# Token halves of 272 and 240 instead of 256 and 256 at the layer boundaries and around the layer norm, in a kernel of two fused transformer blocks

## The chip, the cores and the metric

The kernel runs on one core of one Trainium2 chip. The metric is the time of one execution on the device in microseconds, as the median of several runs. The engines are TensorE (PE in the profile; its weight loads are PEld), VectorE (DVE), ScalarE (ACT), GpSimd (POOL) and SyncE (SP, whose queue carries most of the DMA).

## What is computed

512 tokens of width 1024 pass through two blocks of layers. The first block has two layers, each of them a mixer and a squared-ReLU MLP with an RMS norm before and after ("sandwich"); the mixer of layer 0 is a gated short convolution beside a multi-head attention, that of layer 1 a convolution module with a layer norm inside. The second block is one layer with another attention, pooling and a gated MLP.

```python
for i in range(DEPTH):
    g = sandwich_gains[i]
    h = rms_norm(x, g[0])
    m = parallel_conv_mla(h, ...) if i % 2 == 0 else conformer_conv(h, ...)
    x = x + rms_norm(m, g[1])
    h = rms_norm(x, g[2])
    x = x + rms_norm(squared_relu_mlp(h, mlp_w1[i], mlp_w2[i]), g[3])

def conformer_conv(h, w_pw1, b_pw1, w_dw, b_dw, ln_g, ln_b, w_pw2, b_pw2):
    a, g = jnp.split(h @ w_pw1 + b_pw1, 2, axis=-1)
    u = depthwise_conv(a * jax.nn.sigmoid(g), w_dw) + b_dw
    return jax.nn.silu(layer_norm(u, ln_g, ln_b)) @ w_pw2 + b_pw2
```

What matters here is the line `x = x + rms_norm(m, g)`, followed by the next norm and the next matrix product. It occurs four times, after each mixer and each MLP of the first block. Everything is in float32.

## The kernel before

Activations lie transposed: a tile has 128 channels on its partitions and the 512 tokens along its free dimension, eight tiles to a tensor. A float32 product is made of three matmuls on numbers split into a rounded high part and the rest: high weights by high and low activations, low weights by high activations (`mm3`, L357 to L359). So each activation tile is split before it is used (`split`: ScalarE writes the high part, L397 or, with a scale, L400; VectorE writes the rest, L398 or L401), and so is each block of four 128x128 weight tiles, which arrives as `raw` by DMA and is copied by ScalarE (L284) and subtracted by VectorE (L286; by GpSimd for one stretch of blocks) into a `W` buffer.

The four joints between the layers of the first block are written once, in `boundary`. There the mean of squares over the 1024 channels of `m` is needed for every token before `x` can be updated, and the updated `x` before the next layer's products can start. The tokens are therefore cut in two halves, `LA` (L58) and `LB` (L63), of 256 each:

- The last three output tiles of the old layer (`tile`) are made for LA first, 72 matmuls, then for LB. Each tile is evacuated from PSUM by the caller's `evac` (after the MLPs VectorE adds, L1058; after the mixers ScalarE copies, L923 or L1219) and squared; the squares of the first two are added to `acc` (L469 on ScalarE, L470 on VectorE), the square of the third stays by itself (L949).
- `sums` adds over the channels with three matmuls: the high part of `acc` (L962), its low part (L963), and the third tile's square (L964, a plain float32 matmul, which the profile shows as two rows). It stands for LA after five of the eight products of the first LB tile, and for LB inside the next layer's first pass, in `hook`.
- `rsqrt` makes the scale of a half (L450 on ScalarE, L420, L422 and L424 on VectorE).
- `update` multiplies m by it (L970 on VectorE) and adds it to x (L973, on GpSimd for all of LA, and for LB on VectorE for tiles 0, 1, 2 and 4); `update2` splits the new x into `h` (L400 on ScalarE, L401 on VectorE).
- The next layer's first four output tiles are made in two passes of 96 matmuls, k outermost (`kouter`): the LA pass, which after k = 2 (`HK`) runs `hook`, so that the sum over LB stands there on TensorE, and then the LB pass.

The conformer's layer norm and the products behind it use the same halves (L1175 to L1222), and so does the last output tile of the kernel (L1688).

Each engine works its own queue off in order and waits on semaphores where it needs another. The program is recorded in the order of the code, and the tile framework's scheduler, which weighs the instructions by their shapes, then sets the order of each engine's queue; so what stands next to what on VectorE and ScalarE at a boundary is not in the code.

Of the kernel before, what the change touches and what calls it, by code (L numbers as in the profile page):

```python
# [54 lines left out]
XA = ()  # L55
XB = (0, 1, 2, 4)
HK = 2
LA = slice(0, 256)  # L58
TABLES = [s.name for s in SETS]
EXP_LN, LN = "natural_log_exp_and_others", "natural_log"  # L60
RSQRT, TRIG = "abs_reciprocal_sqrt_and_small", "trig_and_small"
SIGMOID, SILU = "sigmoid_and_others", "silu_and_others"
LB = slice(256, 512)  # L63

# [173 lines left out]

class Weights:
# [58 lines left out]
class Program:  # L304
# [624 lines left out]
    def boundary(self, x, m, acc, last, gi, nxt, first, extra=None):  # L929
# [5 lines left out]
        V, A, G, mm = nc.vector, nc.scalar, nc.gpsimd, nc.tensor.matmul  # L935
        self.norm_set = RSQRT
        self.tables(RSQRT)
        r, acc2 = self.S()[:, :T], self.S()[:, :T]
        h = []
        sq = {}  # L940

        def evac(i, ps, cols):
            o, _, f = last[i]
            f(ps[:, cols], o, cols)
            if i < 2:
                self.square_into(acc[:, cols], m[o][:, cols], False)
            else:
                sq[0] = self.S()[:, :256]
                A.activation(out=sq[0], in_=m[o][:, cols], func=AF.Square)  # L949

        def tile(i, cols, part=slice(0, None), ps=None):
            ps = ps or self.PS()
            for f in last[i][1][part]:
                f(ps[:, cols], cols)
            return ps

        def parts(cols):
            return self.split(self.P(), acc[:, cols], cols=256), sq[0]

        def sums(p, s):  # L960
            ps = self.PS()[:, :256]
            mm(ps, self.ones, p[:, 0, :256], start=True, stop=False)  # L962
            mm(ps, self.ones, p[:, 1, :256], start=False, stop=False)  # L963
            mm(ps, self.onesf, s, start=False, stop=True)  # L964
            return ps

        def update(k, cols):
            if cols is LA:
                h.append(self.P())
            V.scalar_tensor_tensor(out=m[k][:, cols], in0=m[k][:, cols], scalar=self.v("g", 8 * gi + k),  # L970
                                   in1=r[:, cols], op0=OP.mult, op1=OP.mult)
            eng = V if k in (XA if cols is LA else XB) else G
            ins = eng.tensor_add(out=x[k][:, cols], in0=x[k][:, cols], in1=m[k][:, cols]).ins  # L973
            if eng is G:
                self.last_update = ins
# [5 lines left out]
        def updates(ks, cols):  # L981
            ks = list(ks)
            update(ks[0], cols)
            for a, b in zip(ks, ks[1:] + [None]):
                if b is not None:
                    update(b, cols)
                update2(a, cols)

        for i in range(3):
            ps = tile(i, LA)  # L990
            evac(i, ps, LA)
        pb = [tile(0, LB, slice(0, 5))]
        s = sums(*parts(LA))
        tile(0, LB, slice(5, None), pb[0])
        self.rsqrt(s, D, r[:, LA])
        updates(range(4), LA)
        for i in (1, 2):
            pb.append(tile(i, LB))
        for i in range(3):
            evac(i, pb[i], LB)  # L1000
        box = {"p": parts(LB)}

        def hook():
            box["s"] = sums(*box["p"])
            updates(range(4, 8), LA)
            self.rsqrt(box["s"], D, r[:, LB])
            updates(range(8), LB)
            for k in range(8):
                self.square_into(acc2[:, LA], x[k][:, LA], k == 0, G)
            for k in range(8):  # L1010
                self.square_into(acc2[:, LB], x[k][:, LB], k == 0)

        ps = self.kouter(first, h, None, LA, {HK: hook}, extra and extra[0], range(8))
# [50 lines left out]
    def conformer(self, x, h, ps4, rs, first):  # L1064
        nc = self.nc
        V, A, G, mm, W = nc.vector, nc.scalar, nc.gpsimd, nc.tensor.matmul, self.W
# [105 lines left out]
        self.tables(RSQRT)  # L1172

        order = LN_ORDER
        mean = [self.PS()[:, :256] for _ in range(2)]  # L1175

        def means(i):
            for c in order:
# [1 line left out]

        means(0)
        h2 = [self.P() for _ in range(8)]
        sq = [self.PS()[:, :256] for _ in range(2)]
        mus = {}

        def squares(i, cs):
            cols = (LA, LB)[i]
            if i not in mus:
                mus[i] = self.S()[:, :256]
                A.activation(out=mus[i], in_=mean[i], func=AF.Copy, scale=1.0 / D)  # L1190
            for c in cs:
                V.tensor_sub(out=vv[c][:, cols], in0=vv[c][:, cols], in1=mus[i])
                t = self.S()[:, :256]
                A.activation(out=t, in_=vv[c][:, cols], func=AF.Square)
                mm(sq[i], self.onesf, t, start=c == 0, stop=c == 7)

        def normal(i):
            cols = (LA, LB)[i]
            r = self.S()[:, :256]
            self.rsqrt(sq[i], D, r)  # L1200
            self.tables(SILU)
            for c in range(8):
                y = vv[c][:, cols]
                V.tensor_mul(out=y, in0=y, in1=r)
                self.fn(SILU, out=y, in_=y, func=AF.Silu, scale=self.v("lng", c), bias=self.v("lnb", c))
                self.split(h2[c], y, cols=cols)
# [536 lines left out]
```

## Time and profile before

| | |
|---|---|
| median of 3 runs | 1763.58 us (1763.04 to 1767.39) |
| the profiled execution | 1762.84 us |
| its span, first to last instruction | 1761.1 us |
| mean granted TensorE clock | 0.991 |
| TensorE busy | 1724.0 us (98% of the span) |
| VectorE, ScalarE, GpSimd busy | 1091.2, 801.6, 274.0 us |
| share of TensorE in the chain that ended last | 81% |

The times of all rows are microseconds from the start of the span, of the one profiled execution. A row of the timeline gives the start, the duration, the engine, the line, the operation with its output and inputs, the shape, and in brackets the idle time ahead of it with the instruction that ended it. Durations of matmuls contain the way through the array, so neighbours overlap; what a matmul costs is read from the distance of the starts. The four boundaries lie at about 229 to 265, 586 to 623, 794 to 830 and 1152 to 1190 us.

### The profile page before, as it was taken

The numbers are of one execution on the slowest core, as the hardware profiler recorded it, in microseconds if no ns is written. First come the engines' busy times: TensorE is split into PE (matmuls) and PEld (weight loads), VectorE is DVE, ScalarE is ACT, GpSimd is POOL, SyncE is SP. The second block draws the span as 40 slices with busy tenths as digits, with TensorE's granted clock in tenths as the row PEclk, the third lists the DMA queues.
The fourth block names the chain that finished last, engine by engine and source line by source line (L and its number), as shares of the span: only waits on it lengthen the run. The fifth ranks groups of instructions, "written<-read, shape, count | busy, mean of one in ns | idle before, by whom it ended". The sixth has DMA issues, their size and how long they took to land.

```text
span 1761.1 us, 23142 instructions
## 1 busy us (share of the span) xinstructions
PE 1724.0 (98%) x8828; PEld 1460.4 (83%) x8828; DVE 1091.2 (62%) x1772; ACT 801.6 (46%) x1461; POOL 274.0 (16%) x339
## 2 busy tenths in 40 slices
PE   9999999999999999999999999989999999999999
PEld 7778898888888878999888888888787888888887
DVE  7988786344444789968544444488897655344452
ACT  6546655333333446676533333357665443232331
POOL 3513330000000365503000000051223200000000
PEclk9999999999999999999999999999999999999999
DMA  5231313222222133512322222222223222222221
GB/s 198 73 104 55 108 51 130 96 96 96 96 96 96 48 108 107 169 60 85 109 97 96 96 96 96 96 96 74 73 62 101 100 97 98 96 96 96 96 96 60
DMA packets 49887, 167.26 MB, mean 95 GB/s; under 512 B 6848, under 2 KB 7296, under 8 KB 49776
## 3 DMA queue, kind: packets, MB, share of 16 engines
q1 hardware_dynamic: 47776, 160.70, 27.9%
q0 software_dynamic: 1936, 5.07, 0.9%
q8 instruction: 69, 1.13, 0.3%
q14 instruction: 42, 0.34, 0.1%
q10 hardware_dynamic: 64, 0.02, 0.0%
HBM read 158.25 MB, written 4.19 MB: 92 GB/s over the span
## 4 chain that ended last, share of the span: by engine, by line
PE 81%; DVE 11%; issue 3%; ACT 2%; POOL 2%; DMA 1%; SPq 0%; POOLq 0%; ACTq 0%; DVEq 0%
PE ps L357 26%; PE ps L358 26%; PE ps L359 26%; DVE P L970 1%; PE ps L625 1%; DVE W L286 1%; POOL P L973 1%; DVE P L401 1%; DVE S L1479 1%; DVE S L424 1%; DVE P L398 1%; DVE S L422 1%; DMA raw<-in_w 1%; ACT S L450 0%; DVE S L420 0%
## 5 line engine op out<-in xcount | busy, mean ns | idle before, releaser
L357 PE MATMUL ps<-P,W 128*128 128x512 f32 (+1 forms) x2541 | 928.7, 366 | 4.9 <-DVE S L1132 2.8
L358 PE MATMUL ps<-P,W 128*128 128x512 f32 (+1 forms) x2541 | 925.7, 364 | 4.9 <-DVE P L401 4.9
L359 PE MATMUL ps<-P,W 128*128 128x512 f32 (+1 forms) x2541 | 923.9, 364 | 0.0
L284 ACT ACTIVATE W<-raw 128x512 fp32r<-128x512 f32 x578 | 356.6, 628 | 649.9 <-PE ps L359 608.5
L286 DVE TENSOR_TENSOR W<-raw,W 128x512 fp32r<-128x512 f32 x523 | 371.0, 717 | 378.7 <-ACT W L284 376.1
L357 PEld LDWEIGHTS ps<-P,W 128*128 128x128 f32 x2541 | 482.6, 190 | 82.5 <-DVE S L1132 3.2
L358 PEld LDWEIGHTS ps<-P,W 128*128 128x128 f32 x2541 | 482.7, 190 | 79.9 <-DVE P L401 5.7
L359 PEld LDWEIGHTS ps<-P,W 128*128 128x128 f32 x2541 | 482.6, 190 | 75.3 <-DVE W L286 0.2
L973 POOL TENSOR_TENSOR P<-P 128x256 f32<-128x256 f32 x48 | 46.7, 981 | 770.6 <-DVE P L970 769.5
L398 DVE TENSOR_TENSOR P<-S,P 128x512 fp32r<-128x512 f32 (+3 forms) x134 | 93.8, 706 | 50.4 <-ACT P L397 49.8
L397 ACT ACTIVATE P<-S 128x512 fp32r<-128x512 f32 (+3 forms) x134 | 81.5, 614 | 63.8 <-DVE S L1666 25.9
L286 POOL TENSOR_TENSOR W<-raw,W 128x512 fp32r<-128x512 f32 x55 | 72.9, 1348 | 38.1 <-ACT W L284 34.0
L1084 DVE SCALAR_TENSOR_TENSOR ps<-P,vec,ps 128x512 f32<-128x512 f32 x116 | 77.8, 744 | 0.0
L400 ACT ACTIVATE P<-P,vec 128x256 fp32r<-128x256 f32 (+1 forms) x80 | 43.7, 550 | 51.8 <-POOL P L973 31.4
L1031 DVE SCALAR_TENSOR_TENSOR S<-ps,S 128x512 f32<-128x512 f32 x64 | 43.6, 689 | 34.2 <-PE ps L359 34.1
L401 DVE SCALAR_TENSOR_TENSOR P<-P,vec 128x256 fp32r<-128x256 f32 (+1 forms) x80 | 54.3, 692 | 10.9 <-ACT P L400 10.7
L470 POOL TENSOR_TENSOR S<-S 128x256 f32<-128x256 f32 (+1 forms) x45 | 48.7, 1084 | 74.6 <-ACT S L469 72.2
L469 ACT ACTIVATE S<-P 128x256 f32<-128x256 f32 (+1 forms) x105 | 46.4, 472 | 17.4 <-DVE P L1058 11.4
L638 POOL TENSOR_TENSOR P<-S,P 128x512 fp32r<-128x512 f32 (+1 forms) x24 | 34.3, 1427 | 114.4 <-DVE P L637 108.5
L1051 DVE TENSOR_TENSOR P<-ps,P 128x512 f32<-128x512 f32 x42 | 29.0, 691 | 28.7 <-PE ps L359 28.7
L625 PE MATMUL ps<-P 128*128 128x512 f32 (+3 forms) x160 | 41.2, 376 | 2.2 <-DVE S L1445 0.9
L470 DVE TENSOR_TENSOR S<-S 128x256 f32<-128x256 f32 (+1 forms) x60 | 33.1, 551 | 14.4 <-ACT S L469 13.4
(264 smaller groups left out, 1299.8 us busy)
## 6 DMA issues: line engine op xcount, KB each, us to landing
raw<-in_w SPq DMA_DIRECT2D x286, 512.0 KB
P<-in_xT SPq DMA_DIRECT2D x8, 256.0 KB
P<-in_xT POOLq DMA_DIRECT2D x8, 256.0 KB, 5.3
keep<-P SPq DMA_DIRECT2D x8, 256.0 KB
P<-P SPq DMA_DIRECT2D x16, 128.0 KB
P<-keep POOLq DMA_DIRECT2D x8, 256.0 KB, 4.3
out<-P SPq DMA_DIRECT2D x7, 256.0 KB
raw<-in_w SPq DMA_DIRECT2D x2, 256.0 KB
```

The costliest lines, as they stand in the source:

```text
L284: nc.scalar.activation(out=w[:, 0, :cols], in_=r, func=AF.Copy)
L286: eng.tensor_sub(out=w[:, 1, :cols], in0=r, in1=w[:, 0, :cols].bitcast(F32))
L357: mm(ps, w[0], x[0], start=first, stop=False)
L358: mm(ps, w[0], x[1], start=False, stop=False)
L359: mm(ps, w[1], x[0], start=False, stop=last)
L397: nc.scalar.activation(out=hi, in_=src, func=AF.Copy)
L398: nc.vector.tensor_sub(out=lo, in0=src, in1=hi.bitcast(F32))
L401: nc.vector.scalar_tensor_tensor(out=lo, in0=src, scalar=scale, in1=hi.bitcast(F32), op0=OP.mult, op1=OP.subtract)
L470: (eng or nc.vector).tensor_add(out=acc, in0=acc, in1=t)
L625: mm(o[:m], k, q[:, pl, c0:], start=n == 0 and m == 128, stop=n == len(keys) - 1 and mask is None)
L973: ins = eng.tensor_add(out=x[k][:, cols], in0=x[k][:, cols], in1=m[k][:, cols]).ins
L1084: V.scalar_tensor_tensor(out=dst if dst is not None and t == taps[-1] else acc, in0=u, scalar=w, in1=acc, op0=OP.mult, op1=OP.add)
```

## The change

LA takes 272 tokens and LB 240. The widths that were written as 256 follow from the slices, by a new function `size`. It adds four lines above the code of interest, so that a line n of the profile is n + 4 in the changed kernel.

```diff
-LA = slice(0, 256)
+LA = slice(0, 272)
-LB = slice(256, 512)
+LB = slice(272, 512)
...
+def size(cols):
+    return cols.stop - cols.start
...
             else:
-                sq[0] = self.S()[:, :256]
+                sq[0] = self.S()[:, :size(cols)]
...
         def parts(cols):
-            return self.split(self.P(), acc[:, cols], cols=256), sq[0]
+            return self.split(self.P(), acc[:, cols], cols=size(cols))[:, :, :size(cols)], sq[0]
 
         def sums(p, s):
-            ps = self.PS()[:, :256]
-            mm(ps, self.ones, p[:, 0, :256], start=True, stop=False)
-            mm(ps, self.ones, p[:, 1, :256], start=False, stop=False)
+            ps = self.PS()[:, :s.shape[-1]]
+            mm(ps, self.ones, p[:, 0], start=True, stop=False)
+            mm(ps, self.ones, p[:, 1], start=False, stop=False)
             mm(ps, self.onesf, s, start=False, stop=True)
...
-        mean = [self.PS()[:, :256] for _ in range(2)]
+        mean = [self.PS()[:, :size(cols)] for cols in (LA, LB)]
...
-        sq = [self.PS()[:, :256] for _ in range(2)]
+        sq = [self.PS()[:, :size(cols)] for cols in (LA, LB)]
...
-                mus[i] = self.S()[:, :256]
+                mus[i] = self.S()[:, :size(cols)]
...
-                t = self.S()[:, :256]
+                t = self.S()[:, :size(cols)]
...
-            r = self.S()[:, :256]
+            r = self.S()[:, :size(cols)]
```

TensorE's order stays as it was at the boundaries. The queues of VectorE and ScalarE are arranged anew at all four boundaries. Three places show it.

ScalarE at the first boundary, from the last weight copy or split ahead of the second four updates to the rsqrt of LB. `ps_2273` is the third tile's second half, `S_2307` its square, `P_2309` the split of `acc` for LB; P_2356 to P_2377 are h[4] to h[7] for LA, each of which needs its GpSimd addition. Before:

```order
L284 ACTIVATE W_2245<-raw_2158 128x512
L400 ACTIVATE P_2233<-P_1946,vec_82 128x256
L923 ACTIVATE P_1944<-ps_2273 128x256
L949 ACTIVATE S_2307<-P_1944 128x256
L397 ACTIVATE P_2309<-S_1957 128x256
L400 ACTIVATE P_2356<-P_1947,vec_82 128x256
L400 ACTIVATE P_2359<-P_1947,vec_82 128x256
L400 ACTIVATE P_2367<-P_1948,vec_82 128x256
L400 ACTIVATE P_2377<-P_1948,vec_82 128x256
L450 ACTIVATE S_2063<-ps_2352,eps_84 128x256
```

After:

```order
L401 ACTIVATE P_2309<-S_1957 128x240
L288 ACTIVATE W_2238<-raw_2121 128x512
L404 ACTIVATE P_2356<-P_1947,vec_82 128x272
L404 ACTIVATE P_2359<-P_1947,vec_82 128x272
L404 ACTIVATE P_2367<-P_1948,vec_82 128x272
L404 ACTIVATE P_2377<-P_1948,vec_82 128x272
L288 ACTIVATE W_2245<-raw_2158 128x512
L927 ACTIVATE P_1944<-ps_2273 128x240
L953 ACTIVATE S_2307<-P_1944 128x240
L454 ACTIVATE S_2063<-ps_2352,eps_84 128x240
```

The third tile's evacuation and its square have moved from ahead of the four splits into h[4] to h[7] to behind them, with two weight copies now ahead of them as well.

VectorE at the first boundary, from the end of the rsqrt of LA. P_2212 to P_2233 are h[0] to h[3]; P_1652, P_1721 and P_1906 hold m. Before:

```order
L424 SCALAR_TENSOR_TENSOR S_2063<-S_2207,S_2063 128x256
L970 SCALAR_TENSOR_TENSOR P_1652<-P_1652,vec_82,S_2063 128x256 x2
L286 TENSOR_TENSOR W_2220<-raw_2084,W_2220 128x512
L401 SCALAR_TENSOR_TENSOR P_2212<-P_1945,vec_82,P_2212 128x256
L970 SCALAR_TENSOR_TENSOR P_1721<-P_1721,vec_82,S_2063 128x256
L401 SCALAR_TENSOR_TENSOR P_2215<-P_1945,vec_82,P_2215 128x256
L286 TENSOR_TENSOR W_2230<-raw_2121,W_2230 128x512
L970 SCALAR_TENSOR_TENSOR P_1721<-P_1721,vec_82,S_2063 128x256
L401 SCALAR_TENSOR_TENSOR P_2223<-P_1946,vec_82,P_2223 128x256
L286 TENSOR_TENSOR W_2238<-raw_2121,W_2238 128x512
L286 TENSOR_TENSOR W_2245<-raw_2158,W_2245 128x512
L401 SCALAR_TENSOR_TENSOR P_2233<-P_1946,vec_82,P_2233 128x256
```

After:

```order
L428 SCALAR_TENSOR_TENSOR S_2063<-S_2207,S_2063 128x272
L974 SCALAR_TENSOR_TENSOR P_1652<-P_1652,vec_82,S_2063 128x272 x2
L974 SCALAR_TENSOR_TENSOR P_1721<-P_1721,vec_82,S_2063 128x272 x2
L405 SCALAR_TENSOR_TENSOR P_2212<-P_1945,vec_82,P_2212 128x272
L405 SCALAR_TENSOR_TENSOR P_2215<-P_1945,vec_82,P_2215 128x272
L405 SCALAR_TENSOR_TENSOR P_2223<-P_1946,vec_82,P_2223 128x272
L405 SCALAR_TENSOR_TENSOR P_2233<-P_1946,vec_82,P_2233 128x272
L474 TENSOR_TENSOR S_1957<-S_1957,S_2299 128x240
L974 SCALAR_TENSOR_TENSOR P_1906<-P_1906,vec_82,S_2063 128x272
L290 TENSOR_TENSOR W_2220<-raw_2084,W_2220 128x512
```

The four multiplications and the four low parts of LA stand together, and the weight splits that stood between them come later.

VectorE at the second boundary, around the evacuation of the second and third tile for LB (`ps_4946`, `ps_4971`); P_5007 is the split of `acc` for LB, P_5054 to P_5075 are h[4] to h[7] for LA. Before:

```order
L470 TENSOR_TENSOR S_4611<-S_4611,S_4997 128x256
L1058 TENSOR_TENSOR P_2824<-ps_4946,P_2824 128x256
L1058 TENSOR_TENSOR P_2824<-ps_4971,P_2824 128x256
L970 SCALAR_TENSOR_TENSOR P_2823<-P_2823,vec_82,S_4761 128x256
L470 TENSOR_TENSOR S_4611<-S_4611,S_5001 128x256
L970 SCALAR_TENSOR_TENSOR P_2823<-P_2823,vec_82,S_4761 128x256
L970 SCALAR_TENSOR_TENSOR P_2824<-P_2824,vec_82,S_4761 128x256
L398 TENSOR_TENSOR P_5007<-S_4611,P_5007 128x256
```

After:

```order
L1062 TENSOR_TENSOR P_2824<-ps_4946,P_2824 128x240
L474 TENSOR_TENSOR S_4611<-S_4611,S_5001 128x240
L290 TENSOR_TENSOR W_4936<-raw_4819,W_4936 128x512
L402 TENSOR_TENSOR P_5007<-S_4611,P_5007 128x240
L405 SCALAR_TENSOR_TENSOR P_5054<-P_1947,vec_82,P_5054 128x272
L405 SCALAR_TENSOR_TENSOR P_5057<-P_1947,vec_82,P_5057 128x272
L405 SCALAR_TENSOR_TENSOR P_5065<-P_1948,vec_82,P_5065 128x272
L405 SCALAR_TENSOR_TENSOR P_5075<-P_1948,vec_82,P_5075 128x272
L290 TENSOR_TENSOR W_4943<-raw_4856,W_4943 128x512
L1062 TENSOR_TENSOR P_2824<-ps_4971,P_2824 128x240
```

The third tile's evacuation has moved from ahead of the split of `acc` to behind it, the four low parts and a weight split. The third boundary is arranged like the first (with L1219 for L923), the fourth like the second.

## Rows read from the trace of the kernel before

**Rows 1.** The page: span, and TensorE's busy time, share and instructions

```profile
span 1761.1 us, 23142 instructions
...
PE 1724.0 (98%) x8828; PEld 1460.4 (83%) x8828; DVE 1091.2 (62%) x1772; ACT 801.6 (46%) x1461; POOL 274.0 (16%) x339
```

**Rows 2.** Waits of TensorE: who waited for whom; us in total, times, longest

```profile
PE ps L963 <- DVE P L398: 5.2, 4, 1.3
PE ps L358 <- DVE P L401: 4.9, 4, 2.2
PE ps L962 <- ACT P L397: 3.8, 4, 1.7
```

**Rows 3.** Timeline of TensorE at the first boundary: sum over LB, and second pass

```profile
240.65 0.39 PE L962 MATMUL ps<-P,ones 128*128 128x256 f32 x1 [0.21 <-ACT P L397]
242.33 0.39 PE L963 MATMUL ps<-P,ones 128*128 128x256 f32 x1 [1.29 <-DVE P L398]
242.56 0.90 PE L964 MATMUL ps<-S,onesf 128*128 128x256 f32 x2
242.89 0.77 PE L357 MATMUL ps<-P,W 128*128 128x256 f32 x1
...
252.99 0.39 PE L358 MATMUL ps<-P,W 128*128 128x256 f32 x1 [1.02 <-DVE P L401]
```

**Rows 4.** Stages: length, busy us and count by engine, granted clock, DMA share, GB/s

```profile
242.70:246.10 3.40, 3.40 (x17) 3.23 (x16) 2.23 (x6) 1.65 (x5) 1.07 (x2) 0.50 0.00 0
252.99:264.50 11.51, 11.51 (x96) 11.51 (x97) 11.47 (x23) 7.71 (x18) 3.81 (x4) 1.00 0.21 61
990.00:1010.00 20.00, 20.00 (x90) 16.57 (x89) 10.35 (x15) 9.32 (x16) 0.00 (x0) 1.00 0.32 105
```

**Rows 5.** Timeline of TensorE at the second and fourth boundary

```profile
601.53 0.78 PE L357 MATMUL ps<-P,W 128*128 128x256 f32 x1
...
611.12 0.39 PE L358 MATMUL ps<-P,W 128*128 128x256 f32 x1 [0.59 <-DVE P L401]
...
1178.63 0.39 PE L358 MATMUL ps<-P,W 128*128 128x256 f32 x1 [2.20 <-DVE P L401]
```

**Rows 6.** Timeline of TensorE: narrow matmuls of the second block's attention

```profile
1261.05 0.27 PE L358 MATMUL ps<-P 128*128 128x160 f32 x1
...
1261.27 0.22 PE L357 MATMUL ps<-P 128*128 128x32 f32 x1
```

**Rows 7.** Timeline of ScalarE at the first boundary

```profile
234.89 0.36 ACT L923 ACTIVATE P<-ps 128x256 f32<-128x256 f32 x1
...
236.38 0.62 ACT L284 ACTIVATE W<-raw 128x512 fp32r<-128x512 f32 x1
...
238.37 0.42 ACT L949 ACTIVATE S<-P 128x256 f32<-128x256 f32 x1
...
245.38 0.46 ACT L450 ACTIVATE S<-ps,eps 128x256 f32<-128x256 f32 x1
...
256.70 0.91 ACT L400 ACTIVATE P<-P,vec 128x256 fp32r<-128x256 f32 x2 [0.79 <-POOL P L973]
```

**Rows 8.** Timeline of VectorE at the first and second boundary

```profile
232.10 1.22 DVE L286 TENSOR_TENSOR W<-raw,W 128x512 fp32r<-128x512 f32 x1
...
239.00 0.41 DVE L470 TENSOR_TENSOR S<-S 128x256 f32<-128x256 f32 x1
239.34 0.47 DVE L970 SCALAR_TENSOR_TENSOR P<-P,vec,S 128x256 f32<-128x256 f32 x1
...
587.79 0.42 DVE L1058 TENSOR_TENSOR P<-ps,P 128x256 f32<-128x256 f32 x1
...
589.11 1.75 DVE L970 SCALAR_TENSOR_TENSOR P<-P,vec,S 128x256 f32<-128x256 f32 x3
...
594.01 1.28 DVE L286 TENSOR_TENSOR W<-raw,W 128x512 fp32r<-128x512 f32 x2
```

**Rows 9.** Timeline of GpSimd at the first boundary

```profile
231.87 2.05 POOL L973 TENSOR_TENSOR P<-P 128x256 f32<-128x256 f32 x2 [25.53 <-DVE P L970]
234.67 0.91 POOL L973 TENSOR_TENSOR P<-P 128x256 f32<-128x256 f32 x1 [0.75 <-DVE P L970]
```

## The prediction

> **What bounds the kernel now.** I read the page first. TensorE is busy for 98% of the span of 1761.1 us [rows 1], so the time moves only if a matmul takes longer or shorter, if TensorE waits, or if its clock is not granted. The list of who waited for whom comes next: three of TensorE's waits are at the four boundaries and nowhere else, 5.2 us on L963, 4.9 on L358 and 3.8 on L962, four times each, 13.9 us together [rows 2]. TensorE's timeline shows them in place. At the first boundary the column sums of the second half begin at 240.65, their second matmul waits 1.29 us for VectorE's split at L398, the next layer's matmuls go on at 242.89, and at 252.99 the first matmul that needs the second half of h[0] waits 1.02 us for L401 [rows 3]. The table by stage adds a third loss: in the 3.4 us from 242.70 the granted clock is 0.50, the lower of the two levels, right after TensorE had stood still, and 17 matmuls run where 28 fit at the spacing of the second pass (96 in 11.51 us, 0.120 each); that loses some 1.3 us [rows 4]. The second and fourth boundary look the same, with 0.59 and 2.20 us at the later wait [rows 5]; the third then has about 1.1, what is left of the 4.9.
>
> So a boundary is a chain that runs over VectorE, ScalarE and GpSimd, with TensorE waiting for it twice. What the change does to that chain decides, and the order rows show that it does more than alter widths.
>
> **The change, part by part.** *Matmul widths.* In each half 263 products of three matmuls change, so 789 get 16 columns more and 789 get 16 fewer. From 512 columns (90 in 20.00 us, 0.222 each) to 256 (0.120) a column costs 0.0004 us, 16 of them 0.0064 [rows 4]. With 272 columns that makes 0.126, with 240 it makes 0.114: the pair costs as before, and the sum is 0. One end of this: narrow matmuls have a floor, since with 160 columns they still start 0.11 apart (1261.05 to 1261.27 is two steps) [rows 6]. 0.114 lies above it. Were 240 columns no faster than 256, the second half would give nothing back, 789 x 0.0064 = +5.0 us; were they at the floor of 0.11, 789 x 0.004 = -3.2 us. I take 0, since 0.114 is nearer to the floor that is measured than to 0.120. The Trainium skill (TensorE: Matmul & The Clock Gate, section "LDWEIGHTS (loading the stationary operand)") gives a weight load as its columns over 1.2 ns, 107 ns for 128 columns; by its section "Back-to-back issue gap" 256 columns need 109 ns and 240 need 102.5, so the load would hold the narrower half, and the sum would be an estimated +3.5 us instead of 0. The measured 0.11 agrees with its floor; no row here has 240 columns.
>
> *Order at the first and third boundary.* Before, ScalarE evacuated the third tile's second half (L923) and squared it (L949) as soon as the first four updates were through, at 238.4 [rows 7], some two microseconds before TensorE began that sum. Now both stand behind four more L400, each of which needs its GpSimd addition, and two weight copies. The third matmul of the second sum reads that square, so TensorE must wait for it. Worked out from 231.87, where the first addition starts (times are those of the trace before): four additions at 0.96 (1.02 in the pair, 0.91 alone [rows 9]) end at 235.75; the fourth L400 0.51 (256.70: the next starts 0.4 later), 236.25; L923 0.36 and the square 0.42, 237.0 [rows 7]; VectorE's L470 0.41 and L970 0.47, 237.9; a weight split L286, 0.64 alone and 1.22 beside GpSimd, taken as 1.0, 238.9; three L970 beside GpSimd 1.75, 240.65; a second split 1.0 and the second L470 0.41, 242.05 [rows 8]; L397 as long as a square, 242.5; a weight copy L284 0.62, 243.1; four L400 in 1.7, 244.8; L284 0.62, L923 0.36, L949 0.42, 246.2. Neighbours in a queue overlap by up to 0.07 (L470 takes 0.41, its successor starts 0.34 later [rows 8]), over some 15 steps less 0.3 where the step is not handed to another engine: 245.9. In the old run the sum's last matmul started 0.33 before the next layer went on; so TensorE goes on at 246.25 instead of 242.89 [rows 3], **+3.4 us**. The ends: with every split alone and additions at 0.91 the square ends at 245.0 (+2.5); with every split at 1.22 and additions at 1.02, 246.6 (+4.1).
>
> *Order at the second and fourth boundary.* Here VectorE evacuates (L1058). L1058 and one split no longer stand ahead of the first L970: between 587.79 and 589.11 only one instruction of 0.42 remains, so the updates start some 0.9 us earlier, at 588.2 [rows 8]. Then the same chain: additions from 588.8 to 592.6, L400 and L401 to 593.6, L1058 0.42, L970 0.47, split 1.0, L470 0.41, three L970 1.75, split 0.8, L1058, square and L470 1.25, L284 and L397 with it 0.7, 600.4; four L400 1.7, L284 0.62, the split 0.7, the last L1058 0.42 and the square 0.42: 604.25. TensorE goes on at 604.6 instead of 601.53 [rows 5], **+3.0 us**.
>
> *What the later wait gives back.* The first split of the second half depends on the same sum, and its chain from the sum on is as long as before but for one more L970 ahead of it (0.6 to 0.9): at the first boundary rsqrt (L450) starts at some 246.4 instead of 245.38 [rows 7], so h[0] is there about 1.0 + 0.8 later than at 252.99, at 254.8. TensorE itself gets there at 252.99 - 1.02 + 3.4 + 0.4 = 255.8. So the later wait vanishes and is deducted: 1.02, 0.59, 1.1, 2.20 [rows 3, 5].
>
> *Widths on the path.* The 72 matmuls ahead of the chain +0.46, the 15 of the other half ahead of the first sum -0.1, the 60 between sum and second pass +0.38, the 96 of the second pass -0.61, the chain's steps, slightly longer in the first half and shorter in the second, +0.1: together +0.2 per boundary. The 57 + 36 matmuls that lie ahead of the wait are hidden by it.
>
> *Costed at nothing.* The layer norm's sums and squares: wide ones +, narrow ones - on TensorE, which is busy there; without that cover 0.3 us. The last tile of the kernel: 21 matmuls of either width. The weight splits that now come after the second pass's updates: hidden by that pass of 11.5 us [rows 4], as each block of four weight tiles is worth 12 matmuls; if one came late, a wait of about a split and a copy, 1.3 us. The reordered GpSimd splits and the one DMA that changes its place on the SP queue are under the same cover. The clock: I leave the stretch at 0.50 as long as it is.
>
> **Sum:** first 3.4 - 1.0 + 0.2 = 2.6, second 3.0 - 0.6 + 0.2 = 2.6, third 3.4 - 1.1 + 0.2 = 2.5, fourth 3.0 - 2.2 + 0.2 = 1.0: **+8.7 us**. The profiled execution took 1762.84 us, so 1771.5; the median of the runs, 1763.58, stands 0.74 above it, so **1772.3**. With the chain's ends (-0.9 and +0.7 in each boundary) 1768.7 to 1775.1.
>
> **The rivals.** (a) *The waits only change places.* If VectorE and GpSimd run faster when fewer splits lie between the updates (a split beside an addition cost 1.22 where it takes 0.64 alone), the square is done not at 245.9 but near 244, and the first wait grows by no more than the later one shrinks, 1.0 to 1.5 us: 1762 to 1768. For it: the splits do slow the additions, and the first four updates come up to 3 us sooner. Against it: the eight additions, the four L400 behind L397 and the two copies remain, whatever their speed. (b) *Faster.* TensorE loses 13.9 us to these waits and some 5 us to the clock. If ScalarE reaches L949 at most 1.0 us after the moment at which the old run went on with the sum's last matmul (242.56 plus 1.0), the later wait pays for all of it, and the sooner updates and the wider first pass, 60 x 0.0064 = 0.4, are left as gain, at most the 4.9 us of L358 over four boundaries: 1759 to 1763. Against it: 2.3 us of the chain would have to go. (c) *Narrow matmuls gain nothing, or the longer standstill costs clock.* The first is the +5.0 us above; the second a further stretch at 0.50 at each boundary, 1.3 us x 4 = 5.2 us, since TensorE now stands still for some 5.5 us instead of 2 to 3.5. Either one on top: 1777. (The Trainium skill's rule on weight loads, above, speaks for a part of the first.) For it: the clock fell after each of these waits. Against it: where TensorE stands still the low clock costs nothing, so a second stretch need not fall on work. (d) *The order on the chip is the one the rows show but the path lies elsewhere*, so that nothing moves: 1763.6; it is counted with (a).
>
> **How the numbers follow.** Forecast 0.54; (a) with (d) 0.21; (b) 0.12; (c) 0.13. A measurement of this kernel tells about 0.3%, 5.3 us, from no change. The forecast's own range, 1768.7 to 1775.1, is nearly all slower than 1768.9; (c) is slower too; (a) is mostly within; (b) half faster by more than 0.3%, which is below 1758.3, and half within. So slower 0.67, same 0.26, faster 0.07. The range takes in the forecast, (a), the slower part of (b) and most of (c): 1761 to 1778.
>
> **What would show it.** In the profile after: the 128x272 matmuls near 0.126 apart and the 128x240 near 0.114; TensorE's wait on L968 (was L964) for the square at L953 as its longest wait at the boundaries, going on 3 us later after the first sum than now; the wait on L362 (was L358) gone or below half a microsecond at the first three boundaries; four additions on GpSimd in one run after each first rsqrt. The forecast is wrong if L968 has no wait, if the whole difference lies in the spacing of the narrow matmuls, or if a weight split becomes the releaser of a long wait in the second pass.

## The result and the profile after

The changed kernel takes 1771.79 us (median of 6 runs, 1769.95 to 1776.83), the kernel before in the same series 1763.31 us. The ratio is 1.0051, with a 95% interval of 1.0032 to 1.0069: slower by 8.5 us, where 1772.3 us was predicted. The profiled execution took 1776.83 us, the longest of the six; so not its total is compared with the median, but its stages with the stages before. Three single executions of the runs below took far longer than all others (9797.98 and 2420.16 us, and 9340.94 us of the kernel before); the ratios leave them out.

First the page: TensorE's work is as long as before, the span is not [rows 1].

```profile
span 1775.1 us, 23148 instructions
...
PE 1722.4 (97%) x8828; PEld 1457.9 (82%) x8828; DVE 1095.5 (62%) x1772; ACT 803.2 (45%) x1461; POOL 273.4 (15%) x339
```

The list of waits of TensorE (who waited for whom; us in total, times, longest) names the places. A line n of before is n + 4 here, so these answer to [rows 2]:

```profile
PE ps L966 <- ACT P L401: 12.8, 4, 3.5
PE ps L968 <- ACT S L953: 9.6, 4, 2.7
...
PE ps L967 <- DVE P L402: 0.6, 2, 0.3
...
PE ps L362 <- DVE P L405: 0.3, 1, 0.3
```

Before, the sum's first two matmuls waited 3.8 and 5.2 us and the second pass 4.9, together 13.9. Now the sum waits 23.0 us, nearly all of it at its first and its third matmul, and the second pass waits for nothing: the 0.3 us on L362 lie at 13.0 us, in the first layer.

How long a boundary takes is read from TensorE's timeline: from the first 256-wide matmul (272-wide here) to the first 512-wide one behind the second pass; the fourth window runs on to the eighth 512-wide matmul of the next layer, 1.6 us further in both kernels. The table by stage cuts there; its columns are length, busy us and count of PE, PEld, DVE, ACT and POOL, granted clock, DMA share, GB/s. The four boundaries before:

```profile
218.02:264.48 46.46, 43.94 (x345) 43.10 (x344) 39.47 (x70) 26.85 (x63) 16.88 (x19) 0.96 0.16 50
575.04:622.78 47.74, 44.13 (x345) 43.18 (x344) 38.84 (x66) 23.21 (x53) 22.46 (x23) 0.96 0.14 45
783.80:830.27 46.47, 43.89 (x345) 43.17 (x344) 37.33 (x66) 27.04 (x62) 16.63 (x19) 0.96 0.19 60
1141.08:1194.78 53.70, 48.55 (x386) 46.54 (x385) 42.72 (x79) 28.49 (x61) 28.36 (x44) 0.97 0.30 99
```

and after:

```profile
221.47:270.63 49.16, 43.80 (x346) 42.94 (x344) 39.90 (x70) 25.29 (x60) 17.07 (x19) 0.93 0.13 44
581.42:631.88 50.46, 43.99 (x346) 43.19 (x345) 39.46 (x70) 21.99 (x52) 19.22 (x28) 0.93 0.13 41
795.19:843.88 48.69, 43.97 (x345) 43.07 (x344) 38.56 (x67) 26.10 (x61) 16.70 (x19) 0.93 0.17 55
1154.71:1210.01 55.30, 48.89 (x387) 46.86 (x385) 43.19 (x77) 26.35 (x59) 27.89 (x44) 0.94 0.26 88
```

The differences are +2.70, +2.72, +2.22 and +1.60 us, +9.24 in all. The first window starts 3.45 us later than before, although up to there both kernels run the same instructions in the same order; in the profiles of this case that start lies anywhere from 217.7 to 222.6, whatever the kernel. It belongs to the run, not to the change. Of the 14.0 us between the two spans, 3.45 lie there, 9.24 at the boundaries, and 2.2 between the second boundary and the conformer's convolution, where the gates are made (below); elsewhere 0.9 are gained.

TensorE at the first boundary, against [rows 3]:

```profile
246.92 0.57 PE L966 MATMUL ps<-P,ones 128*128 128x240 f32 x1 [2.99 <-ACT P L401]
247.36 0.57 PE L967 MATMUL ps<-P,ones 128*128 128x240 f32 x1
250.30 1.17 PE L968 MATMUL ps<-S,onesf 128*128 128x240 f32 x2 [2.37 <-ACT S L953]
250.93 0.76 PE L361 MATMUL ps<-P,W 128*128 128x272 f32 x1
...
253.89 0.28 PE L361 MATMUL ps<-P,W 128*128 128x272 f32 x1
...
259.91 0.27 PE L361 MATMUL ps<-P,W 128*128 128x240 f32 x1
260.01 0.28 PE L362 MATMUL ps<-P,W 128*128 128x240 f32 x1
```

With the 3.45 taken off, the sum begins 2.8 us later than before, the next layer goes on 4.6 us later, and the second pass, which waited 1.02 us, finds h[0] ready. What stands ahead of the two late operands is seen on ScalarE,

```profile
240.26 0.41 ACT L473 ACTIVATE S<-P 128x240 f32<-128x240 f32 x1
...
246.46 0.40 ACT L401 ACTIVATE P<-S 128x240 fp32r<-128x240 f32 x1 [4.06 <-DVE S L474]
...
247.29 1.75 ACT L404 ACTIVATE P<-P,vec 128x272 fp32r<-128x272 f32 x4
...
249.84 0.40 ACT L953 ACTIVATE S<-P 128x240 f32<-128x240 f32 x1
```

on VectorE,

```profile
235.07 2.77 DVE L974 SCALAR_TENSOR_TENSOR P<-P,vec,S 128x272 f32<-128x272 f32 x4
...
242.04 2.35 DVE L974 SCALAR_TENSOR_TENSOR P<-P,vec,S 128x272 f32<-128x272 f32 x3
244.31 1.24 DVE L290 TENSOR_TENSOR W<-raw,W 128x512 fp32r<-128x512 f32 x1
245.47 0.95 DVE L474 TENSOR_TENSOR S<-S 128x240 f32<-128x240 f32 x1
...
259.05 0.46 DVE L405 SCALAR_TENSOR_TENSOR P<-P,vec 128x240 fp32r<-128x240 f32 x1
```

and beside it on GpSimd.

```profile
235.66 3.75 POOL L977 TENSOR_TENSOR P<-P 128x272 f32<-128x272 f32 x4 [25.86 <-DVE P L974]
...
243.13 3.04 POOL L977 TENSOR_TENSOR P<-P 128x272 f32<-128x272 f32 x3 [0.38 <-DVE P L974]
```

The square (L953) stands behind four L404 and two weight copies, as the order rows said. The split of the sum (L401) waits for the second L474, which stands behind three multiplications and a weight split that take 0.78 and 1.24 us each while GpSimd adds.

### The profile page after: what moved, and what is told of

Read it like the earlier page. It is cut to its first block, busy times and chain, and to the rows that moved or that the text cites. A ratio compares the mean times of both kernels' runs of the same rounds, so it can differ in the third digit from the quotient of the medians.

```text
span 1775.1 us, 23148 instructions
## 1 busy us (share of the span) xinstructions
PE 1722.4 (97%) x8828; PEld 1457.9 (82%) x8828; DVE 1095.5 (62%) x1772; ACT 803.2 (45%) x1461; POOL 273.4 (15%) x339
## 4 chain that ended last, share of the span: by engine, by line
PE 80%; DVE 12%; issue 3%; ACT 3%; DMA 1%; POOL 1%; SPq 0%; ACTq 0%; DVEq 0%; POOLq 0%
PE ps L361 26%; PE ps L362 25%; PE ps L363 25%; DVE W L290 2%; PE ps L629 1%; DVE P L974 1%; DVE P L405 1%; DMA raw<-in_w 1%; ACT W L288 1%; DVE P L402 1%; DVE S L1483 1%; DVE S L428 1%; ACT S L454 1%; DVE S L426 1%; DVE S L424 0%
## 5 line engine op out<-in xcount | busy, mean ns | idle before, releaser
L361 PE MATMUL ps<-P,W 128*128 128x512 f32 (+3 forms) x2541 | 927.4, 365 | 7.6 <-DVE S L1136 4.0
L362 PE MATMUL ps<-P,W 128*128 128x512 f32 (+3 forms) x2541 | 922.7, 363 | 0.3 <-DVE P L405 0.3
L363 PE MATMUL ps<-P,W 128*128 128x512 f32 (+3 forms) x2541 | 922.0, 363 | 0.0
L362 PEld LDWEIGHTS ps<-P,W 128*128 128x128 f32 x2541 | 481.0, 189 | 75.3 <-DVE P L405 0.6
L977 POOL TENSOR_TENSOR P<-P 128x272 f32<-128x272 f32 (+1 forms) x48 | 45.7, 970 | 757.3 <-DVE P L974 757.3
L401 ACT ACTIVATE P<-S 128x512 fp32r<-128x512 f32 (+3 forms) x134 | 81.6, 615 | 68.7 <-DVE S L1670 25.9
L474 POOL TENSOR_TENSOR S<-S 128x272 f32<-128x272 f32 (+1 forms) x45 | 49.4, 1098 | 97.6 <-ACT S L473 95.4
L404 ACT ACTIVATE P<-P,vec 128x272 fp32r<-128x272 f32 (+2 forms) x80 | 42.4, 548 | 46.8 <-POOL P L977 29.4
L473 ACT ACTIVATE S<-P 128x272 f32<-128x272 f32 (+2 forms) x105 | 47.0, 474 | 24.7 <-DVE P L1062 18.6
L405 DVE SCALAR_TENSOR_TENSOR P<-P,vec 128x272 fp32r<-128x272 f32 (+2 forms) x80 | 51.6, 675 | 4.3 <-ACT P L404 4.2
L974 DVE SCALAR_TENSOR_TENSOR P<-P,vec,S 128x272 f32<-128x272 f32 (+1 forms) x64 | 44.4, 733 | 0.3
```

Source lines behind the costliest of these rows:

```text
L361: mm(ps, w[0], x[0], start=first, stop=False)
L362: mm(ps, w[0], x[1], start=False, stop=False)
L363: mm(ps, w[1], x[0], start=False, stop=last)
L401: nc.scalar.activation(out=hi, in_=src, func=AF.Copy)
L405: nc.vector.scalar_tensor_tensor(out=lo, in0=src, scalar=scale, in1=hi.bitcast(F32), op0=OP.mult, op1=OP.subtract)
L474: (eng or nc.vector).tensor_add(out=acc, in0=acc, in1=t)
```

## The experiments

Three theories. **A**: the order of the queues at the boundaries costs the time. **B**: the unequal widths cost it. **C**: the layer norm does. The table gives all runs; the length is the sum of the four boundaries, cut as above from each run's own timeline. Where a diff has `self.after(a, b)`, instruction a is made to stand behind b; it adds an order and no work.

| run | LA, LB | ratio to before (95%) | median us | length us |
|---|---|---|---|---|
| before | 256, 256 | 1 | | 194.37 |
| the change | 272, 240 | 1.0051 (1.0032 to 1.0069) | 1771.79 | 203.61 |
| order_258_254 | 258, 254 | 1.0038 (1.0026 to 1.0051) | 1769.71 | 201.82 |
| mirror_240_272 | 240, 272 | 1.0052 (1.0039 to 1.0064) | 1771.92 | 192.71 |
| mirror_norm_256 | 240, 272 | 1.0014 (1.0004 to 1.0024) | 1764.73 | 193.38 |
| norm_only | 256, 256 | 0.9998 (0.9986 to 1.0009) | 1761.23 | 194.43 |
| square_first | 272, 240 | 1.0028 (1.0018 to 1.0039) | 1767.10 | 197.04 |
| sum_first_272 | 272, 240 | 1.0021 (1.0011 to 1.0030) | 1765.55 | |
| order_back_272 | 272, 240 | 1.0004 (0.9994 to 1.0015) | 1761.44 | 190.63 |
| sum_first_258 | 258, 254 | 1.0044 (1.0030 to 1.0058) | 1769.48 | 197.70 |
| sum_first_256_all | 256, 256 | 1.0004 (0.9995 to 1.0014) | 1762.56 | 197.25 |
| sum_first_256_but_one | 256, 256 | 0.9968 (0.9956 to 0.9981) | 1756.14 | 191.29 |
| squares_late_256 | 256, 256 | 0.9962 (0.9950 to 0.9974) | 1755.67 | 187.04 |
| sum_first_squares_late | 256, 256 | 0.9939 (0.9924 to 0.9954) | 1751.53 | 181.90 |

The medians of before in the three later series are 1761.61, 1760.73 and 1760.94 us; a ratio is to its own series and differs by up to 0.1% from the quotient of the medians. All these differences are under 1%; the intervals tell which of them are clear of zero. The fourth window of the last run ends 2.9 us behind the first 512-wide matmul, not 1.6. Of sum_first_272 there is no usable profile, so it has no length and no rows.

**order_258_254**: the new order with nearly the old widths.

```diff
-LA = slice(0, 272)
+LA = slice(0, 258)
-LB = slice(272, 512)
+LB = slice(258, 512)
```

> LA takes 258 tokens and LB 254. The widths are nearly those before (2 columns of 789 + 789 matmuls, +0.6 and -0.6 us), but VectorE's and ScalarE's queues at the boundaries stand in the order of the changed kernel: the third tile's second half is evacuated and squared behind the splits into h[4] to h[7]. Theory A (the order of the queues costs the time): the first and the third matmul of the sum over LB wait as in the changed kernel, some 20 us or more over four boundaries, the later wait on L362 is below 1 us, and the time is 1769 to 1774. Theory B (the widths cost it: longer chain and matmuls in the first half): no long wait on L968, 1762 to 1765. Theory C (the layer norm's unequal halves cost it): 1762 to 1765 too.

The ratio of 1.0038 is 6.7 us, against 9.0 us by the ratio of the change. The waits of TensorE are the changed kernel's:

```profile
PE ps L966 <- ACT P L401: 10.7, 4, 3.1
PE ps L968 <- ACT S L953: 10.2, 4, 2.6
```

Theory A holds, B and C fall as the main cause: two tokens more in LA are enough for 6.7 of the 9.0 us, and the intervals of the two kernels overlap. Of the four pairs run here, the two with 254 or 240 in LB are arranged the new way, those with 256 or 272 the old way. What in the scheduler draws that line was not tried.

**mirror_240_272**, with `LA = slice(0, 240)` and `LB = slice(240, 512)`, and **norm_only**, with slices of their own for the layer norm:

```diff
+NA, NB = slice(0, 272), slice(272, 512)
...
-        mean = [self.PS()[:, :size(cols)] for cols in (LA, LB)]
+        mean = [self.PS()[:, :size(cols)] for cols in (NA, NB)]
```

> LA takes 240 tokens and LB 272, the same two widths in the other halves. The queues at the boundaries stand as before the change (the third tile's evacuation and square ahead of the splits into h[4] to h[7]). Theory A (order): the waits are those of before, 5.2 us and 3.8 us on the first two matmuls of the sum, none above 0.5 us on the third; the shorter first pass (60 matmuls of 0.0064 us less) lets the later wait grow by some 0.4 us per boundary and the longer last tiles cover the first half's chain; 1761 to 1767. Theory B (widths): unequal halves cost about the same whichever comes first, 1769 to 1774.

> 256 and 256 at the boundaries and in the last tile of the kernel, 272 and 240 in the layer norm and the two passes behind it alone. Theory A: boundaries as before, the layer norm moves nothing by more than 1 us: 1762 to 1765. Theory C (the layer norm carries a part of the loss): 1766 to 1771.

The mirror missed: it is as slow as the change. But its boundaries are not long (192.71). The time went into the layer norm, which takes 6.8 us more there, from the last products ahead of it to the end of its second pass; TensorE's timeline has it in one row:

```profile
763.45 2.18 PE L1199 MATMUL ps<-S,onesf 128*128 128x272 f32 x4 [4.47 <-ACT S L1198]
```

The second half's sums of squares stand behind only 17 matmuls of the first pass on TensorE's own queue there, where the change and the kernel before have 56 and 58, and wait at its head for squares that ScalarE makes later. An order again, in another place. norm_only shows the layer norm of 272 and 240 to cost nothing that can be measured (0.1 us in its profile).

**mirror_norm_256**: the mirror with 256 and 256 in the layer norm.

```diff
+NA, NB = slice(0, 256), slice(256, 512)
```

> 240 and 272 at the boundaries, 256 and 256 in the layer norm. In the mirror run the layer norm alone cost some 6.6 us, since there TensorE's sums of squares of the second half (L1199) stood early in its queue and waited 4.5 us, and its boundaries some 3 us. Theory A (the order did it, there in TensorE's queue): the layer norm costs nothing now, the boundaries keep their 3 us (a shorter first pass covers less of the second half's chain): 1763 to 1766. Theory B (unequal halves at the boundaries cost it): 1768 to 1772.

The layer norm's loss is gone, as theory A says. The 3 us that this expectation gave the boundaries do not show: with 240 and 272 tokens in the old order they are no longer than before (193.38 against 194.37). What remains, 0.14% or 2.5 us, is of the size of what the conformer's gates, from the second boundary to the first 256-wide matmul of the convolution, take more, 2.6 us (73.13 against 70.54); TensorE waits 4.0 us instead of 2.8 there, and the granted clock is 0.95 instead of 0.98.

**square_first**: one part of the order undone.

```diff
-                A.activation(out=sq[0], in_=m[o][:, cols], func=AF.Square)
+                sq[1] = A.activation(out=sq[0], in_=m[o][:, cols], func=AF.Square).ins
...
+            if k == 4 and cols is LA:
+                self.after(self.head, sq[1])
```

> 272 and 240 with one part of the order undone: the splits into h[4] to h[7] of LA stand behind the square of the third tile of LB again; all else as in the changed kernel. Theory A with the square as the cause of the second wait: the wait on L968 falls from 9.6 us to under 3 us, the wait on L966 (12.8 us) stays, because the sum of the first two squares is still late on VectorE; the later wait takes back at most 0.5 us per boundary; 1763 to 1768. Rival (the wait only changes place, to the later wait on L362 or to h[4] in the first pass): 1769 to 1773.

```profile
PE ps L966 <- ACT P L401: 12.7, 4, 3.5
...
PE ps L968 <- ACT S L953: 2.6, 4, 0.8
```

As expected of theory A: 7.0 us of wait go, the other wait stays, and the boundaries shorten by 6.6 us (203.61 to 197.04).

**sum_first_272** and **order_back_272** undo the rest. `tail_lb` is the low part of the LB sum; order_back_272 has `k >= 5`, and also puts the multiplications behind the third tile's evacuation where VectorE makes that (`sq[2]`).

```diff
+            if k >= 4 and cols is LA:
+                self.after(mul, self.tail_lb)
+                if sq[2]:
+                    self.after(mul, sq[2])
```

> 272 and 240, both parts of the order undone: as square_first, and besides the multiplications of the second four updates of LA stand behind the low part of the LB sum on VectorE, so that no GpSimd addition and no multiplication lies ahead of the sum's two parts. Theory A (order alone, widths cost under 2 us): the wait on L966 falls from 12.7 us to under 3 us and that on L968 stays under 5 us (two weight copies still stand ahead of the third evacuation on ScalarE); the later wait on L362 comes back with 0.5 to 1 us per boundary; 1757 to 1763, at or below the time before. Rival (the sum is late for another reason, or the splits into h[4] to h[7] become the next wait in the first pass): 1765 to 1768, as square_first.

> 272 and 240 with the order undone as far as it goes: the third square ahead of the splits into h[4] to h[7], the multiplications for h[5] to h[7] behind the sum's low part and behind the third tile's evacuation on VectorE (after the MLPs). Theory A (nearly all of the loss is order): waits on L966, L967 and L968 together under 12 us as before, 1759 to 1764. Theory B (what is left after the order is the widths): 1765 to 1769 whatever the waits on the sum.

The first has the rival's time. What held it is not shown; sum_first_258, below, has the same edges and one more, and shows the third evacuation behind the multiplications. With that put ahead too, the second takes the time of the kernel before, with 272 and 240 tokens:

```profile
PE ps L362 <- DVE P L405: 6.8, 7, 1.6
...
PE ps L968 <- ACT S L953: 3.4, 4, 1.0
...
PE ps L966 <- ACT P L401: 1.5, 3, 0.7
...
PE ps L967 <- DVE P L402: 0.6, 2, 0.3
```

The sum waits 5.5 us instead of 23.0, the later wait is back (4.9 of the 6.8 us on L362; 1.6 more are for late splits in the first pass), and the ratio is 1.0004. So the loss is the order, and at the boundaries the widths cost nothing: their length is 190.63 us. The order is not that of the kernel before, though. The sum waits less than it did there (9.0 us), so the boundaries are 3.7 us shorter, and the ratio is still 1.0004. In the profile 1.6 us of this lie in the stretch of the gates (72.09 us against 70.54). sum_first_256_but_one, below, has much the same edges with 256 and 256 tokens: its boundaries are as long (191.29), that stretch is 3.7 us shorter (68.43), and its ratio is 0.9968. Whether the widths or, again, an order made that stretch longer was not tried.

**sum_first_258**, **sum_first_256_all** and **sum_first_256_but_one** carry the finding over to a faster kernel: the LB sum ahead of the second four multiplications (from k = 4 in the first two, from k = 5 in the third), and the rsqrt of LB ahead of the splits into h[6] and h[7].

```diff
-            updates(range(4, 8), LA)
+            update(4, LA)
+            update(5, LA)
+            update2(4, LA)
+            update(6, LA)
+            update2(5, LA)
+            update(7, LA)
             self.rsqrt(box["s"], D, r[:, LB])
+            sq[2] = self.table_fns[-1]
+            update2(6, LA)
+            update2(7, LA)
...
+            if k == 6 and cols is LA:
+                self.after(self.head, sq[2])
```

> 258 and 254 (so the weight splits come late and the first four updates stand together, as in the changed kernel), square first, sum first, and the rsqrt of LB ahead of the splits into h[6] and h[7]. Theory A: no wait at the boundaries above 1 us but that on L968 for the third square behind two weight copies; 1755 to 1761. Rival (a weight split that was put off stops the first pass): waits on L361 for W of 1 us and more at the boundaries, 1762 to 1767.

> 256 and 256 in the order before, with the second four multiplications of LA behind the low part of the LB sum, and the rsqrt of LB on ScalarE ahead of the splits into h[6] and h[7]. If TensorE's waits at the boundaries are set by what stands ahead of the sum on VectorE, the wait on L967 (5.2 us) falls to under 2 us, L966 (3.8 us) to under 2 us, the wait on L362 stays under 5 us because the rsqrt starts sooner: 1754 to 1760. Rival: h[4] is now too late for the first pass (its multiplication starts 1.3 us later), a wait on h[4] of some 0.5 to 1.5 us per boundary takes the gain back: 1760 to 1764.

> As sum_first_256_all, but the multiplication for h[4] stays ahead of the sum's low part and only those for h[5] to h[7] stand behind it. If h[4] was the limit there, this one is faster by 1 to 4 us; if not, it is slower by up to 2 us, since one GpSimd addition stands beside the sum's low part. 1754 to 1761.

sum_first_258 met neither theory as it was put. After the MLPs the third tile's evacuation (L1077, on VectorE) still stood behind the four multiplications, and TensorE waited 4.1 us for it. Its boundaries are 4.1 us shorter than those of order_258_254 (197.70 against 201.82), yet its ratio is no lower; 2.0 us are lost again in the stretch of the gates (72.63 against 70.65), the rest is not explained. VectorE and TensorE at the second boundary:

```profile
604.03 2.62 DVE L974 SCALAR_TENSOR_TENSOR P<-P,vec,S 128x258 f32<-128x258 f32 x4
...
607.71 0.41 DVE L1077 TENSOR_TENSOR P<-ps,P 128x254 f32<-128x254 f32 x1
```

```profile
608.68 1.22 PE L968 MATMUL ps<-S,onesf 128*128 128x254 f32 x2 [4.13 <-ACT S L953]
```

In sum_first_256_all the rival won: the sum waits 1.8 us over the four boundaries instead of 9.0, but h[4] is late, the first of three waits behind the sum at the first boundary, where the kernel before has one.

```profile
247.72 0.39 PE L362 MATMUL ps<-P,W 128*128 128x256 f32 x1 [1.05 <-DVE P L405]
```

Leaving one multiplication ahead of the sum (sum_first_256_but_one) gives 0.32% against before. The later wait on L362 is 8.0 us there; the next two runs go for it.

**squares_late_256** moves GpSimd's sums of squares of LA away from VectorE's first updates of LB, and **sum_first_squares_late** joins it with sum_first_256_but_one.

```diff
+            if k == 7:
+                sq[4] = ins
...
-                self.square_into(acc2[:, LA], x[k][:, LA], k == 0, G)
+                self.square_into(acc2[:, LA], x[k][:, LA], k == 0, G, sq[4])
```

> 256 and 256 in the order before, but GpSimd's seven additions of squares of LA stand behind its last update of LB instead of beside VectorE's first updates of LB. Theory (VectorE takes about twice as long beside GpSimd): the multiplications for LB ahead of the first splits fall from 0.87 us to 0.47 each, the additions from 0.92 to 0.41, h[0] of LB is there some 1.7 us sooner, the wait on L362 falls from 4.9 us to under 1.5 us: 1756 to 1760. Rival (the durations on VectorE have another cause): the rows stay, 1760 to 1763. Rival (the squares come too late for the next layer): a wait of TensorE behind the second pass, 1762 to 1768.

> sum_first_256_but_one and squares_late_256 together. If the later wait of sum_first_256_but_one (8.0 us on L362) comes from VectorE beside GpSimd, it falls to under 3 us: 1749 to 1754. If it stays or the squares come late: 1755 to 1762.

VectorE before, with GpSimd's squares (from 246.52 on, 0.88 each) beside it:

```profile
247.70 1.73 DVE L970 SCALAR_TENSOR_TENSOR P<-P,vec,S 128x256 f32<-128x256 f32 x2
```

and in squares_late_256, where they start at 259.36:

```profile
249.08 0.88 DVE L976 SCALAR_TENSOR_TENSOR P<-P,vec,S 128x256 f32<-128x256 f32 x2
249.88 0.75 DVE L979 TENSOR_TENSOR P<-P 128x256 f32<-128x256 f32 x2
```

A multiplication takes 0.44 us instead of 0.87, the wait on L362 falls from 4.9 to 0.7 us, and the kernel is 0.38% faster than before. Both edits together make 0.61%, 1751.53 us: faster than both kernels of this study.

## Why the prediction was right

**The total and its place.** The sum was +2.6, +2.6, +2.5 and +1.0 over the boundaries, 8.7 in all; their lengths grew by 2.70, 2.72, 2.22 and 1.60, 9.24. That the order did it, and not the widths, is shown from both sides: order_258_254 has the loss at nearly the old widths, and mirror_norm_256 and order_back_272 have unequal widths and boundaries that are no longer than before (193.38 and 190.63 against 194.37).

**The terms are less exact than the sum.** The forecast let TensorE go on 3.4 us later at the first boundary, and 0.4 more for the widths ahead of that; it was 4.6 (250.93 less 3.45 and 242.89). Measured from the start of each window, TensorE goes on 4.6, 3.8, 4.1 and 4.0 us later, where 3.8, 3.4, 3.8 and 3.4 were worked out, some 2 us too little in all; from there on 7.3 us are given back, where the forecast had some 5.5. The two errors cancel in the sum, and that is luck. The working of the chain holds up to the first square (done at 237.2 by the trace less 3.45, 237.0 in the text). It fails at "three L970 beside GpSimd 1.75" and "a second split 1.0 and the second L470 0.41": measured 2.35, 1.24 and 0.95, all beside the additions that now stand in one run. The first split took less, 0.69 instead of 1.0. From the first addition (235.66) to the end of the second L474 that makes 10.8 us instead of 10.2, and it is why L966 and not, as foretold, L968 has the longest wait. The first addition itself is 0.3 us later, behind the wider last tiles. From there to the square the chain is as worked out (3.4 us from the end of L401 to the end of L953, 3.4 in the text with the overlaps taken off). The rest came at the end: L968 to the next layer took 0.63 us at the low clock, 0.33 before.

**What gave it back.** The later wait went as forecast, at all four boundaries. At the first, VectorE ends h[0]'s low part at 259.51, TensorE comes at 260.01, 0.5 us later, where 1.0 had been worked out. The second pass gave back 0.9 us instead of the 0.61 foretold (10.62 from 260.01 to 270.63, 11.49 before), because 240 columns are quicker than estimated.

**The widths.** Read over 48 and 96 steps of the timeline, matmuls of 272 columns start 0.125 apart (253.89 to 259.91) and of 240 columns 0.112 (259.91 to 270.63), against 0.126 and 0.114 foretold; with 256 columns the same pass before had 0.120 [rows 4]. So 240 columns come close to the 0.11 seen at 160 [rows 6], and the pair is an estimated 789 x 0.008 less 789 x 0.005, some 2 us, cheaper on TensorE where nothing covers it: between the prediction's 0 and its lower bound of -3.2. The Trainium skill (TensorE: Matmul & The Clock Gate, section "Back-to-back issue gap") has 256 columns at 109 ns, as the gap of a matmul by itself, which made the pair an estimated 3.5 us dearer; here, in a stream with a weight load to each matmul, 256 columns take 120 ns [rows 4], so the trace does not bear out that price, while the weight load of the same page's section "LDWEIGHTS (loading the stationary operand)", 107 ns, is close to the 0.112. The profile's own rows of weight loads last 0.19 us (mean on L357 before), longer than the distance of their starts, so they overlap and do not give that figure.

**The clock.** Rival (c) had a second stretch at the low clock cost up to 1.3 us per boundary. The stretch came, but on the standstill: at the first boundary the granted clock is 0.50 for 6.83 us instead of 3.41, of which only 2.83 us fall on work of the next layer. In these, 11 of its matmuls start, where before it were 14; the counts of the table, 14 below and 17 in [rows 4] and in the prediction, take in rows of the sum as well. At 0.120 the 14 would have taken 1.7 us instead of 3.3, so the low clock cost 1.6 us before, not the 1.3 of the prediction, and costs an estimated 1.5 now (2.83 less 11 x 0.125).

```profile
246.92:253.75 6.83, 4.46 (x15) 3.90 (x16) 5.01 (x10) 5.54 (x15) 0.99 (x2) 0.50 0.23 77
250.93:253.76 2.83, 2.83 (x14) 2.77 (x12) 1.68 (x3) 2.26 (x7) 1.00 (x2) 0.50 0.01 1
```

**What was costed at nothing and was not.** Ahead of the conformer's gates TensorE waits 4.0 us (2.8 before), for the rsqrt that closes the second boundary. TensorE, VectorE and GpSimd there:

```profile
647.37 0.79 PE L361 MATMUL ps<-P,W 128*128 128x512 f32 x1 [4.00 <-DVE S L1136]
```

```profile
643.01 1.85 DVE L426 SCALAR_TENSOR_TENSOR S<-S 128x512 f32<-128x512 f32 x1
644.89 1.63 DVE L428 SCALAR_TENSOR_TENSOR S<-S 128x512 f32<-128x512 f32 x1
```

```profile
640.52 7.13 POOL L290 TENSOR_TENSOR W<-raw,W 128x512 fp32r<-128x512 f32 x5 [0.67 <-ACT W L288]
```

The two steps took 0.69 us each before; now five weight splits run on GpSimd beside them. This adds 1.2 us of wait, and behind the wait the clock stays low for longer, so that the stretch of the gates, before and after, is 2.2 us longer:

```profile
622.78:693.32 70.54, 67.71 (x292) 55.50 (x291) 62.38 (x94) 32.54 (x52) 37.14 (x47) 0.98 0.33 105
631.88:704.58 72.70, 68.70 (x292) 56.29 (x291) 62.68 (x92) 34.33 (x55) 41.09 (x42) 0.95 0.31 102
```

The forecast had these GpSimd splits under cover, so this was missed; the layer norm, costed at nothing too, took 0.15 us more. The boundaries and this stretch make 11.4 us in the one profiled execution, the medians differ by 8.5. That the median came out within 0.5 us of the forecast is therefore partly luck: the runs of one kernel differ by 7 us, more than what was missed.

## What to carry to other kernels

Where a scheduler arranges the queues by shapes, a change of a size is first a change of order: compare the queues before costing the columns, and look for the last operand of whatever the busiest engine waits for. Here two tokens cost 6.7 us, and sixteen cost nothing that could be told once the operands of the sum were put ahead by hand. An edge that puts the operand of the next wait ahead of work with slack was worth more here than either size: three such edges made this kernel 0.61% faster, and of the two numbers of multiplications that were left ahead of the sum, one and none, one was the better.

## What was not expected of the hardware

VectorE beside GpSimd came down to GpSimd's pace: with the sums of squares beside them its multiplications take 0.87 us against 0.44 alone, while each of GpSimd's additions takes 0.88. The Trainium skill (SBUF — State Buffer, section "SBUF: two separate sides") says that a VectorE instruction with two SBUF inputs and a GpSimd instruction that reads SBUF lock each other out: the one that starts first has the port for the whole of its time. The trace agrees that VectorE is held up. It does not show the sum of both times, 0.44 + 0.88 = 1.32 us per pair, but one VectorE instruction to each of GpSimd's: seven beside seven from 246.52 to 252.65 before.

With shorter waits at the sum, TensorE's clock did not fall at all at the first three boundaries of sum_first_squares_late. TensorE stands 0.21 and 1.72 us there ahead of the first and the second sum, and nowhere for long behind them. The granted clock of these stretches is 1.00, the upper of its two levels throughout (mean 0.96 before, 0.93 after the change), so a part of its gain is clock and not wait. The first two:

```profile
221.41:264.05 42.64, 42.35 (x345) 41.70 (x344) 35.97 (x67) 25.10 (x59) 15.11 (x17) 1.00 0.16 51
575.01:619.91 44.90, 42.41 (x345) 41.70 (x344) 35.71 (x66) 21.93 (x50) 18.36 (x19) 1.00 0.14 48
```
